# Up projection of a gated MLP: high and low parts of the operand in one matmul of 512 columns for four of a step's seven products

## The chip, the cores and the metric

The kernel runs on one core of a Trainium2 chip. The metric is the device time of one execution in microseconds (us); it was measured in three runs of the kernel before, and one more execution was recorded by the hardware profiler. TensorE (PE in the profile) does the matmuls and loads their weights (PEld), VectorE (DVE) and ScalarE (ACT) do elementwise work, GpSimd (POOL) and SyncE (SP) here mostly start DMAs.

## The reference, cut to what matters

The reference is one transformer block over 512 tokens of width 2048 in fp32: attention and a short convolution, then a gated MLP with a convolution of three taps along the tokens. The change lies in the MLP, in its first product `h @ w_up`:

```python
D_MODEL = 2048; SEQ = 512
FFN_DIM = ((8 * D_MODEL // 3 + 127) // 128) * 128      # 5504 = 43 * 128

def dwconv3(x, w, b):
    xp = jnp.pad(x, ((0, 0), (1, 1), (0, 0)))
    return xp[:, :-2] * w[0] + xp[:, 1:-1] * w[1] + xp[:, 2:] * w[2] + b

def conv_ffn(h, w_up, cw, cb, w_down):
    u = dwconv3(h @ w_up, cw, cb)
    a, g = jnp.split(u, 2, axis=-1)
    return (a * jax.nn.silu(g)) @ w_down

hf_l = modulate(rms_norm(x, g_ffn_norm[l]), sh_f, sc_f)
x = x + gt_f * conv_ffn(hf_l, w_up[l], ffn_conv_w[l], ffn_conv_b[l], w_down[l])
```

## The kernel before

Every fp32 operand of TensorE is split in two: a rounded part (`h`, high) and what is left (`l`, low). A product is made of three matmuls on top of each other in one bank, `mm3` (lines 185 to 189): high weights with high activations (L187), high weights with low activations (L188), low weights with high activations (L189).

The width 2048 of the normed activations lies in 16 tiles `hf0` to `hf15` of 128 partitions and 512 tokens, each as a high and a low tile. The 43 column tiles of `a` and the 43 of `g` form 43 steps f. The first three are made by plain rows of matmuls over 512 tokens (names `uf`). The other 40 (f = 3 to 42, the loop that begins near line 1199) use a Strassen scheme, in which the tokens are halved (256 each), the width is halved (even and odd tiles) and the two column tiles of the step, one of `g` and one of `a`, are the third pair. A step then needs seven products instead of eight, each over 8 blocks of width and 256 columns: 7 x 8 x 3 = 168 matmuls of 256 columns. The products are named by their activations:

- p1 on "11" (first half of the tokens of the even `hf`), p2 on "21" (first half of the odd `hf`), p6 on "2" and q5 on "1" (sums of halves, the tiles `T`), p7 on "3" (a sum stored over the second half of the even `hf`). These five run in step f itself.
- q4 on "4" (a `T` tile) and q3 on "22" (second half of the odd `hf`) of step f run within step f+1, in `finish`, between p2 and p6 of that step.

Weights of a product come as one tile of 128 x 1024 (eight blocks). `split4` casts them to high on ACT (L998) and subtracts on VectorE for low (L999); there are three buffers each for high and low. In the trace `u27q4h` is the high part of the weights of product q4 of step 27, and u27a, u27b, u27c are the three banks of step 27: a collects p1, p6, p7 and q4, b is p2's, c collects q5 and q3. After p1, p6 and p7 ACT copies bank a aside (L1174). VectorE adds the pieces into the tiles `cg` and `ca` (L1212, L1224, L1182; L1180 on ACT). Then come the convolution (`conv3`: L1005 on ACT, L1006 and L1007 on VectorE), silu (L1013) and the product of `a` and `g` (L1015).

The weights of a step are five tiles: 11, 12, 22, and the sums s1 and s3. SP loads all five (L1119) into nine buffers; for s1 and s3 POOL then starts a second DMA that adds onto the loaded tile (L1121, 512 KB). VectorE makes two more sums from them (L1213, L1214).

The results of two steps make a pair. From f = 7 on, `pair_sums` (L1031 to L1061) writes seven operands of each pair to memory for the down projection, one `put` after another; each call of `pump(1)` behind a product asks for the next one. A put is a cast on ACT (L1042), a subtraction on VectorE (L1043) and a DMA of 256 KB started by POOL (L1044) to `t_d`. The seven, in order, are called #1 to #7 here: "11", "1", "3", "22", "2", "21", "4". In the trace `tp922` is the put of pair 9 (steps 25 and 26) for the operand "22". The tile `tp` of a put comes from the same 58 buffers as `hf` (32) and `T` (24), so two are left: #6 takes the buffer of #4, #7 that of #5, and the second put of the next pair that of #7. POOL starts its DMAs in the order of its instructions, so puts and the adding DMAs of the weights stand in one line.

The order on each engine is not written by hand. A scheduler with an estimate of each instruction's time arranges the program when it is built.

Of the kernel before, what the change touches and what calls it, by code (L numbers as in the profile page):

```python
# [10 lines left out]
F32 = mybir.dt.float32  # L11
F32R = mybir.dt.float32r
# [60 lines left out]
def block_kernel(ctx, tc, xt, ctxt, ctxn, c, c_ctx, w_ada, small, w_in, w_inc, w_q, w_kv, w_out,  # L73
# [23 lines left out]
    def t2(shape, dt, name):  # L97
        return act.tile(shape, dt, tag="t2", bufs=NT2, name=name)
# [80 lines left out]
    def part(w, i, n=1):  # L179
        return tuple(z[:, i * P:(i + n) * P] for z in w)  # L180
# [4 lines left out]
    def mm3(ps, w, x, first, last, on_top=False):  # L185
        with tc.issue_after(behind.pop()) if behind else ExitStack():
            PE.matmul(ps, w[0], x[0], start=first, stop=False, skip_group_check=on_top)  # L187
        PE.matmul(ps, w[0], x[1], start=False, stop=False, skip_group_check=on_top)  # L188
        PE.matmul(ps, w[1], x[0], start=False, stop=last, skip_group_check=on_top)  # L189


    bg, post, late_bg = deque(), [], []
# [437 lines left out]
    with ExitStack() as pb:  # L630
# [238 lines left out]
        def bank_of(i, nm):  # L869
            return p8.tile([P, 512], F32, tag=f"s{i}", bufs=1, name=nm)  # L870
# [41 lines left out]
    def whole(raw, xs, nm, ps=None, cols=slice(0, T), ld=None, often=False):  # L912
# [10 lines left out]
            pump(1)  # L923
        return ps

    hf = {}


    hf_last = [None, None]

    def hf_tile(j, cols=slice(0, T)):
        if j not in hf:
            hf[j] = tuple(t2([P, T], F32R, f"hf{j}{z}") for z in "hl")
        sc = tiny(1, f"fs{j}")
        scale_of(sc, s("g_ffn", j), mod[:, 64 + j:65 + j])
        xr = xres[j][:, cols]
        with tc.issue_after(hf_last[0]) if hf_last[0] is not None else ExitStack():
            V.tensor_tensor(out=xr, in0=xr, in1=rl[:, cols], op=ALU.mult)
        A.activation(xr, xr, AF.Identity, bias=mod[:, 48 + j:49 + j], scale=sc)
        hi, lo = (z[:, cols] for z in hf[j])  # L940
        A.copy(out=hi, in_=xr)
        ins = V.tensor_tensor(out=lo, in0=xr, in1=hi.bitcast(F32), op=ALU.subtract)
        hf_last[:] = hf_last[1], ins.ins

    def hf_early():
# [129 lines left out]
    def t_sums(j):  # L1075

        e, o = xres[2 * j], xres[2 * j + 1]
        i, c = j // 2, HS[j % 2]
        if j % 2 == 0:
            for n in (1, 2, 4):  # L1080
                TT[n, i] = tuple(t2([P, T], F32R, f"T{n}{i}{z}") for z in "hl")

        def put(dst, src):
            hi, lo = dst
            A.copy(out=hi, in_=src)
            V.tensor_tensor(out=lo, in0=src, in1=hi.bitcast(F32), op=ALU.subtract)

        V.tensor_tensor(out=e[:, H0], in0=e[:, H0], in1=e[:, H1], op=ALU.subtract)
        V.tensor_tensor(out=e[:, H1], in0=o[:, H1], in1=e[:, H1], op=ALU.subtract)
        put(half_of(hf[2 * j], 1), e[:, H1])  # L1090
        V.scalar_tensor_tensor(out=o[:, H1], in0=e[:, H0], scalar=-1.0, in1=o[:, H1], op0=ALU.mult, op1=ALU.subtract)
        V.scalar_tensor_tensor(out=o[:, H0], in0=o[:, H1], scalar=-1.0, in1=o[:, H0], op0=ALU.mult, op1=ALU.subtract)
        for n, src in ((1, e[:, H0]), (2, o[:, H1]), (4, o[:, H0])):
            put(tuple(z[:, c] for z in TT[n, i]), src)

    def operand(n, j):
        if n in ("11", "3"):
            return half_of(hf[2 * j], n == "3")
        if n in ("21", "22"):
            return half_of(hf[2 * j + 1], n == "22")  # L1100
        return half_of(TT[int(n), j // 2], j % 2)

    def first_weights(k, held=False):

# [8 lines left out]
    def up_load(f):  # L1113
# [7 lines left out]
                G_.dma_start(r[-1], src[more], accum_op=ALU.add)  # L1121
        return r

    pss = [bank_of(i, f"uf{g}") for g, i in enumerate((2, 3, 4, 5, 1, 0))]
    held = [first_weights(k, k > 2) for k in range(EARLY)]
    for k in range(3, EARLY):
        hf_tile(k, H0)
    for k in range(EARLY):
        row(pss, held[k], hf[k], k, H0)
        pump(1)  # L1130
    drain()
    for k in range(EARLY):
        hf_tile(k, H1)
        row(pss, held[k], hf[k], k, H1)
        pump(1)
        if k in (3, 5):
            t_sums(k // 2 - 1)
# [9 lines left out]
    for k in range(EARLY, NK):  # L1147
        w = nxt
        if k + 1 < NK:
            if k == NK - 4:  # L1150
                raws = up_load(G // 2)
            if k == NK - 2:
                t_sums(sums.popleft())
            nxt = prepare(k + 1)
        row(pss, w, hf[k], k)
        if k % 2:
            sums.append(k // 2)
            t_sums(sums.popleft())
# [3 lines left out]
    bank8 = in_turn(BANKS)  # L1162
    one_bank[0] = bank8

    def product(ps, a, n, nm, first):

        w = split4(a, 1024, nm)
        for j in range(8):
            mm3(ps[:, :256], part(w, j), operand(n, j), first and j == 0, j == 7, on_top=not first)
        pump(1)  # L1170

    def aside(ps, nm):
# [4 lines left out]
    def finish(st):  # L1177
        f, a22, s4, u2, u3, pa, pc, cg, ca = st
        product(pa, a22, "4", f"u{f}q4", False)
        A.activation(ca[:, H0], pa[:, :256], AF.Identity, scale=-1.0)  # L1180
        product(pc, s4, "22", f"u{f}q3", False)
        V.tensor_tensor(out=cg[:, H1], in0=pc[:, :256], in1=u2, op=ALU.add)  # L1182
        acts(f, cg, ca)


# [13 lines left out]
    for f in range(G // 2, NF):  # L1199
        a11, a12, s1, s3, a22 = raws  # L1200
        if f + 1 < NF:
            raws = up_load(f + 1)
        else:
            for _ in range(AHEAD):
                plain_fetch()
        pa, pb, pc = (bank8(f"u{f}{z}") for z in "abc")
        cg = cp.tile([P, T], F32, tag="cg", bufs=2, name=f"cg{f}")
        ca = cp.tile([P, T], F32, tag="ca", bufs=2, name=f"ca{f}")
        product(pa, a11, "11", f"u{f}p1", True)
        u1 = aside(pa, f"u{f}1")  # L1210
        product(pb, a12, "21", f"u{f}p2", True)
        V.tensor_tensor(out=cg[:, H0], in0=pb[:, :256], in1=u1, op=ALU.add)  # L1212
        V.tensor_tensor(out=a11, in0=a11, in1=s1, op=ALU.add)  # L1213
        V.tensor_tensor(out=a12, in0=a12, in1=a11, op=ALU.add)  # L1214
        if pend is not None:
            finish(pend)
        if first_acts and f == G // 2:
            acts(*first_acts.pop(0))
        product(pa, a11, "2", f"u{f}p6", False)
        u2 = aside(pa, f"u{f}2")  # L1220
        product(pc, s1, "1", f"u{f}q5", True)
        product(pa, s3, "3", f"u{f}p7", False)
        u3 = aside(pa, f"u{f}3")
        V.scalar_tensor_tensor(out=ca[:, H1], in0=pc[:, :256], scalar=-1.0, in1=u3, op0=ALU.mult, op1=ALU.subtract)  # L1224
        if first_acts:
            acts(*first_acts.pop(0))
        pend = f, a22, a12, u2, u3, pa, pc, cg, ca
# [366 lines left out]
```

## Time and profile before

| | us |
|---|---|
| median of 3 runs | 2148.93 |
| lowest and highest | 2143.85, 2150.8 |
| the profiled execution | 2158.83 |
| its span, first to last instruction | 2157.0 |

| engine | busy, us | share of the span |
|---|---|---|
| TensorE, matmul | 2104.9 | 98% |
| TensorE, weight load | 1946.7 | 90% |
| VectorE | 1769.0 | 82% |
| ScalarE | 1047.1 | 49% |
| GpSimd | 188.1 | 9% |

The 40 steps lie between about 820 and 1685 us of the span. In the rows of a timeline the first number is the start, the second the duration in us, then follow the engine, the line in the kernel, the operation, and what is written from what; in brackets stands how long the engine was idle before and what ended that. A matmul's shown duration runs until its result is out, so that neighbours overlap; the pace is read from one start to the next. In a row of DMA issues the last number is the time from issue to landing.

### The profile page before, as it was taken

How to read it: one execution, taken by the hardware profiler on the slowest of the kernel's cores; microseconds unless marked ns; L12 is line 12 of the kernel's file. 1: busy time of each engine (PE TensorE's matmuls, PEld its weight loads, DVE VectorE, ACT ScalarE, POOL GpSimd, SP SyncE). 2: the span in 40 equal slices, each digit the busy share in tenths (PEclk: the TensorE clock that was granted, in tenths of full speed). 3: DMA queues.
4: the chain of work that ended last, by engine and by line, in shares of the span. 5: the costliest groups of instructions: out<-in, count | busy, mean ns of one | idle time of the engine just before them, and what ended most of it. 6: DMA issues, size and time to landing. Idle time of an engine off the chain costs nothing.

```text
span 2157.0 us, 37744 instructions
## 1 busy us (share of the span) xinstructions
PE 2104.9 (98%) x14458; PEld 1946.7 (90%) x14458; DVE 1769.0 (82%) x2859; ACT 1047.1 (49%) x1710; POOL 188.1 (9%) x270
## 2 busy tenths in 40 slices
PE   7899999999999999999999999999999999999997
PEld 4688788888888888999999999999999889999997
DVE  7998987778886889788888788788888658888877
ACT  5533333555552237555555555555555333333445
POOL 0000000000000000111211111111111000000000
PEclk9999999999999999999999999999999999999998
DMA  9979785334559986577887877877887999877683
GB/s 335 345 275 337 270 279 176 128 126 162 177 199 348 344 278 192 159 217 201 241 232 215 240 229 220 237 231 219 241 229 218 341 335 290 254 220 236 196 247 111
DMA packets 162121, 513.89 MB, mean 238 GB/s; under 512 B 18962, under 2 KB 23314, under 8 KB 156306
## 3 DMA queue, kind: packets, MB, share of 16 engines
q1 hardware_dynamic: 133364, 418.14, 56.5%
q0 software_dynamic: 27488, 92.29, 18.3%
q8 instruction: 113, 1.85, 0.3%
q10 hardware_dynamic: 1088, 1.05, 0.1%
q14 instruction: 68, 0.56, 0.1%
HBM read 464.22 MB, written 46.14 MB: 237 GB/s over the span
## 4 chain that ended last, share of the span: by engine, by line
PE 86%; DVE 6%; DMA 5%; issue 1%; ACT 1%; SPq 0%; DVEq 0%; POOLq 0%; ACTq 0%
PE pp L187 4%; PE pp L189 4%; PE pp L188 4%; PE o L189 1%; PE o L187 1%; PE o L188 1%; DMA ada<-in_w_ada 1%; PE d L187 1%; PE d L189 1%; PE d L188 1%; PE uf L187 1%; PE uf L188 1%; PE of L187 1%; PE of L188 1%; PE of L189 1%
## 5 line engine op out<-in xcount | busy, mean ns | idle before, releaser
L1044 POOL DMA_DIRECT2D t_d<-tp x126 | 71.9, 574 | 468.3 <-DVE tp L1043 465.4
L255 DVE SCALAR_TENSOR_TENSOR ada<-ada,sv 128x1024 f32<-128x1024 f32 x68 | 82.1, 1219 | 12.1 <-DMA ada<-in_w_ada 12.0
L166 ACT CAST w_0h<-rw 128x512 fp32r<-128x512 f32 (+1 forms) x63 | 38.3, 618 | 108.3 <-PE pp L188 63.1
L1121 POOL DMA_DIRECT2D u_s<-in_w_up x80 | 70.2, 878 | 224.4 <-DMA u_s<-in_w_up 131.5
L233 DVE SCALAR_TENSOR_TENSOR ada<-ada,sv 128x1024 f32<-128x1024 f32 x64 | 77.5, 1217 | 4.4 <-DMA ada<-in_w_ada 3.9
L522 DVE SCALAR_TENSOR_TENSOR ada<-ada,svc 128x1024 f32<-128x1024 f32 x64 | 76.0, 1220 | 2.3 <-DMA ada<-in_w_ada 2.3
L785 POOL TENSOR_TENSOR gr<-gr,half 128x8 f32<-128x8 f32 x4 | 10.1, 2524 | 628.7 <-DVE gr L784 536.8
L1042 ACT CAST tp<-a 128x256 fp32r<-128x256 f32 x90 | 34.7, 405 | 60.5 <-DMA t_d<-tp 54.1
L167 DVE TENSOR_TENSOR w_0l<-rw,w_0h 128x512 fp32r<-128x512 f32 (+1 forms) x63 | 42.6, 681 | 22.3 <-ACT w_0h L166 22.3
L255 DVE SCALAR_TENSOR_TENSOR ra<-ra,sv 128x1024 f32<-128x1024 f32 x44 | 52.5, 1217 | 1.1 <-DMA ra<-in_w_ada 1.1
L1213 DVE TENSOR_TENSOR u<-u,u_s 128x1024 f32<-128x1024 f32 x40 | 48.8, 1219 | 0.7 <-DMA u_s<-in_w_up 0.7
L1214 DVE TENSOR_TENSOR u<-u,u 128x1024 f32<-128x1024 f32 x40 | 48.7, 1218 | 0.0
L1043 DVE TENSOR_TENSOR tp<-a,tp 128x256 fp32r<-128x256 f32 x90 | 36.2, 418 | 12.3 <-ACT tp L1042 12.3
L756 ACT CAST pth<-t 128x384 fp32r<-128x384 f32 x64 | 28.6, 485 | 26.4 <-PE t L753 26.4
L1042 ACT CAST tp<-ts 128x256 fp32r<-128x256 f32 x36 | 14.6, 407 | 43.5 <-DMA t_d<-tp 41.1
L533 DVE TENSOR_TENSOR acc<-acc,pp 128x512 f32<-128x512 f32 x50 | 34.0, 680 | 2.1 <-PE pp L189 2.1
L757 DVE TENSOR_TENSOR ptl<-t,pth 128x384 fp32r<-128x384 f32 x64 | 33.2, 549 | 2.7 <-ACT pth L756 2.7
L737 DVE TENSOR_REDUCE mn<-s 128x1 f32<-128x768 f32 x32 | 30.4, 952 | 4.8 <-PE s L726 4.6
L1043 DVE TENSOR_TENSOR tp<-ts,tp 128x256 fp32r<-128x256 f32 x36 | 15.2, 421 | 23.3 <-ACT tp L1042 23.3
L1005 ACT ACTIVATE g<-cg,sm 128x512 f32<-128x512 f32 x40 | 32.5, 813 | 0.5 <-DVE cg L1182 0.5
L1005 ACT ACTIVATE a<-ca,sm 128x512 f32<-128x512 f32 x40 | 32.1, 803 | 0.0
L1013 ACT ACTIVATE g<-g 128x512 f32<-128x512 f32 x43 | 27.2, 632 | 6.4 <-DVE g L1007 6.4
(15967 smaller groups left out, 9398.2 us busy)
## 6 DMA issues: line engine op xcount, KB each, us to landing
ada<-in_w_ada SPq DMA_DIRECT2D x196, 512.0 KB, 6.0
u<-in_w_up SPq DMA_DIRECT2D x120, 512.0 KB, 8.2
w<-t_d SPq DMA_DIRECT2D x161, 256.0 KB, 5.2
u_s<-in_w_up SPq DMA_DIRECT2D x80, 512.0 KB, 4.3
u_s<-in_w_up POOLq DMA_DIRECT2D x80, 512.0 KB, 8.9
t_d<-tp POOLq DMA_DIRECT2D x126, 256.0 KB, 4.9
v<-in_w_dnw SPq DMA_DIRECT2D x72, 384.0 KB, 5.4
ra<-in_w_ada SPq DMA_DIRECT2D x22, 1024.0 KB, 4.9
```

The lines of the kernel that those rows point to most:

```text
L187: PE.matmul(ps, w[0], x[0], start=first, stop=False, skip_group_check=on_top)
L188: PE.matmul(ps, w[0], x[1], start=False, stop=False, skip_group_check=on_top)
L189: PE.matmul(ps, w[1], x[0], start=False, stop=last, skip_group_check=on_top)
L233: V.scalar_tensor_tensor(out=r, in0=r, scalar=1.0, in1=vec[:, i * 1024:(i + 1) * 1024], op0=ALU.mult, op1=ALU.mult, accum_out=col[:, i:i + 1])
L255: keep(V.scalar_tensor_tensor(out=r, in0=r, scalar=1.0, in1=svs[i], op0=ALU.mult, op1=ALU.mult, accum_out=lc[:, t % 4:t % 4 + 1] if i else ...
L522: keep(V.scalar_tensor_tensor(out=raw[q], in0=raw[q], scalar=1.0, in1=svc[:, q * 1024:(q + 1) * 1024], op0=ALU.mult, op1=ALU.mult, accum_o ...
L1005: A.activation(u, src, AF.Identity, bias=s("fb", m), scale=s("fw", 86 + m))
L1042: A.copy(out=z[:, :256], in_=src)
L1043: V.tensor_tensor(out=z[:, 256:], in0=src, in1=z[:, :256].bitcast(F32), op=ALU.subtract)
L1044: G_.dma_start(t_d[p, OPS.index(n)], z.bitcast(F32))
L1121: G_.dma_start(r[-1], src[more], accum_op=ALU.add)
L1213: V.tensor_tensor(out=a11, in0=a11, in1=s1, op=ALU.add)
```

## The change

For four of the seven products (p2, q5, q4, q3; `APART`) the high and low parts of the operand lie side by side in one tile of 512 columns. A new `mm2` multiplies the high weights with both at once, one matmul of 512 columns: high times high falls into the first half of the bank, high times low into its second half. The low weights then meet the high part in a matmul of 256 columns. Two matmuls take the place of three. What lies in the bank's second half is added by VectorE: `beside`, four new additions or subtractions of 128 x 256 in each step, one behind each of the four products' results.

To have the parts side by side, the odd `hf` tiles and the `T` tiles are laid out by half of the tokens, high beside low. The plain rows of the first three column tiles then do their odd tiles in two halves: 36 matmuls of 256 columns in the place of 18 of 512.

```diff
+    def mm2(ps, w, x, first, last, on_top=False):
+        n = x.shape[1] // 2
+        with tc.issue_after(behind.pop()) if behind else ExitStack():
+            PE.matmul(ps[:, :2 * n], w[0], x, start=first, stop=False, skip_group_check=on_top)
+        PE.matmul(ps[:, :n], w[1], x[:, :n], start=False, stop=last, skip_group_check=on_top)
...
+    def side_by_side(z, src):
+        n = T // 2
+        A.copy(out=z[:, :n], in_=src)
+        return V.tensor_tensor(out=z[:, n:], in0=src, in1=z[:, :n].bitcast(F32), op=ALU.subtract)
...
-        hi, lo = (z[:, cols] for z in hf[j])
-        A.copy(out=hi, in_=xr)
-        ins = V.tensor_tensor(out=lo, in0=xr, in1=hi.bitcast(F32), op=ALU.subtract)
+        if j % 2 == 0:
...
+        else:
+            for h in range(2):
+                if cols in (HS[h], slice(0, T)):
+                    hf[j, h] = t2([P, T], F32R, f"hf{j}{h}")
+                    ins = side_by_side(hf[j, h], xres[j][:, HS[h]])
...
-        if j % 2 == 0:
-            for n in (1, 2, 4):
-                TT[n, i] = tuple(t2([P, T], F32R, f"T{n}{i}{z}") for z in "hl")
+        for n in (1, 2, 4):
+            TT[n, j] = t2([P, T], F32R, f"T{n}{j}")
...
+    def up_row(w, k, hs=(0, 1)):
+        if k % 2 == 0:
+            row(pss, w, hf[k], k, slice(hs[0] * 256, hs[-1] * 256 + 256))
+            return
+        for g in range(G):
+            for h in hs:
+                mm3(pss[g][:, HS[h]], w[g], two(hf[k, h]), False, k == NK - 1 and h == 1)
...
+    APART = ("21", "1", "4", "22")
+
+    def beside(dst, ps, minus=False):
+        V.tensor_tensor(out=dst, in0=dst, in1=ps[:, 256:], op=ALU.subtract if minus else ALU.add)
+
     def product(ps, a, n, nm, first):
         w = split4(a, 1024, nm)
         for j in range(8):
-            mm3(ps[:, :256], part(w, j), operand(n, j), first and j == 0, j == 7, on_top=not first)
+            x = operand(n, j)
+            if n in APART:
+                mm2(ps, part(w, j), x, first and j == 0, j == 7, on_top=not first)
+            else:
+                mm3(ps[:, :256], part(w, j), x if isinstance(x, tuple) else two(x), first and j == 0, j == 7, on_top=not first)
         pump(1)
...
         A.activation(ca[:, H0], pa[:, :256], AF.Identity, scale=-1.0)
+        beside(ca[:, H0], pa, True)
         product(pc, s4, "22", f"u{f}q3", False)
         V.tensor_tensor(out=cg[:, H1], in0=pc[:, :256], in1=u2, op=ALU.add)
+        beside(cg[:, H1], pc)
...
         V.tensor_tensor(out=cg[:, H0], in0=pb[:, :256], in1=u1, op=ALU.add)
+        beside(cg[:, H0], pb)
...
         V.scalar_tensor_tensor(out=ca[:, H1], in0=pc[:, :256], scalar=-1.0, in1=u3, op0=ALU.mult, op1=ALU.subtract)
+        beside(ca[:, H1], pc, True)
```

The change also shifts what the scheduler makes of the program. Lines are numbered higher in the changed kernel: the split is L1023 and L1024, the puts are L1067, L1068 and L1069, the adding DMA is L1144, `beside` is L1200, `mm2` is L196 and L197.

ScalarE in step 28, before, from the cast of p6's weights to the cast of the next step's p1; `ts9` and `a26` are sources of puts of pair 9, `g27` and `a27` begin the convolution of step 27:

```order
L998 CAST u28p6h_14765<-u28_11_14351 128x1024
L1042 CAST tp92_14681<-ts9_14525 128x256
L998 CAST u28q5h_14795<-u28_s1_14355 128x1024
L1180 ACTIVATE ca27_14367<-u27a_14363 128x256
L1042 CAST tp921_14716<-a26_14492 128x256
L998 CAST u28p7h_14823<-u28_s3_14358 128x1024
L1005 ACTIVATE g27_14755<-cg27_14366,sm_82 128x512
L1005 ACTIVATE a27_14760<-ca27_14367,sm_82 128x512
L998 CAST u29p1h_14871<-u29_11_14601 128x1024
```

The same stretch of ScalarE in the changed kernel:

```order
L1023 CAST u28p6h_14158<-u28_11_13793 128x1024
L1023 CAST u28q5h_14188<-u28_s1_13797 128x1024
L1221 ACTIVATE ca27_13809<-u27a_13805 128x256
L1067 CAST tp92_14087<-ts9_13946 128x256
L1023 CAST u28p7h_14208<-u28_s3_13800 128x1024
L1030 ACTIVATE g27_14148<-cg27_13808,sm_82 128x512
L1030 ACTIVATE a27_14153<-ca27_13809,sm_82 128x512
L1067 CAST tp921_14115<-a26_13913 128x256
L1023 CAST u29p1h_14257<-u29_11_14015 128x1024
```

Puts #5 (`tp92`) and #6 (`tp921`) stand about one product later; #6 now stands right ahead of the cast of p1's weights of step 29.

GpSimd around the adding DMAs of step 29 (`u29_s1`, `u29_s3`), before:

```order
L1044 DMA t_d_80<-tp93_14594 128x512
L1044 DMA t_d_80<-tp922_14646 128x512
L1121 DMA u29_s1_14605<-in_w_up 128x1024
L1044 DMA t_d_80<-tp92_14681 128x512
L1121 DMA u29_s3_14608<-in_w_up 128x1024
L1044 DMA t_d_80<-tp921_14716 128x512
L1044 DMA t_d_80<-tp94_14750 128x512
```

The same stretch of GpSimd in the changed kernel:

```order
L1069 DMA t_d_80<-tp93_14007 128x512
L1144 DMA u29_s1_14019<-in_w_up 128x1024
L1069 DMA t_d_80<-tp922_14060 128x512
L1144 DMA u29_s3_14022<-in_w_up 128x1024
L1069 DMA t_d_80<-tp92_14087 128x512
L1069 DMA t_d_80<-tp921_14115 128x512
L1069 DMA t_d_80<-tp94_14142 128x512
```

Put #4 (`tp922`) has moved from ahead of the adding DMA of s1 to behind it, and #5 from ahead of that of s3 to behind it.

TensorE at the passage from q4 to q3 of step 27, before:

```order
L187 MATMUL u27a_14363<-T43h_8334,u27q4h_14688 128x256
L188 MATMUL u27a_14363<-T43l_8335,u27q4h_14688 128x256
L189 MATMUL u27a_14363<-T43h_8334,u27q4l_14689 128x256
L187 MATMUL u27c_14365<-hf1h_7571,u27q3h_14721 128x256
L188 MATMUL u27c_14365<-hf1l_7572,u27q3h_14721 128x256
L189 MATMUL u27c_14365<-hf1h_7571,u27q3l_14722 128x256
```

The same passage in the changed kernel:

```order
L196 MATMUL u27a_13805<-T47_8497,u27q4h_14095 128x512
L197 MATMUL u27a_13805<-T47_8497,u27q4l_14096 128x256
L187 MATMUL u28a_14027<-T20_7910,u28p6h_14158 128x256
L188 MATMUL u28a_14027<-T20_7910,u28p6h_14158 128x256
L196 MATMUL u27c_13807<-hf11_7839,u27q3h_14121 128x512
L197 MATMUL u27c_13807<-hf11_7839,u27q3l_14122 128x256
```

Each group of three has become a group of two, and the first two matmuls of p6 of step 28 now stand ahead of q3. Put orders like these are found in 15 pairs of steps (f = 12 to 40).

More of the change, by code (lines that the diff above doesn't have):

```diff
@@ L926, in block_kernel, with two @@
     hf = {}
+    def side_by_side(z, src):
+        n = T // 2
+        A.copy(out=z[:, :n], in_=src)
+        return V.tensor_tensor(out=z[:, n:], in0=src, in1=z[:, :n].bitcast(F32), op=ALU.subtract)
+    def two(z):
+        return z[:, :T // 2], z[:, T // 2:]
     hf_last = [None, None]
     def hf_tile(j, cols=slice(0, T)):
-        if j not in hf:
+        if j % 2 == 0 and j not in hf:
             hf[j] = tuple(t2([P, T], F32R, f"hf{j}{z}") for z in "hl")
@@ L939, in hf_tile @@
         A.activation(xr, xr, AF.Identity, bias=mod[:, 48 + j:49 + j], scale=sc)
-        hi, lo = (z[:, cols] for z in hf[j])
-        A.copy(out=hi, in_=xr)
-        ins = V.tensor_tensor(out=lo, in0=xr, in1=hi.bitcast(F32), op=ALU.subtract)
+        if j % 2 == 0:
+            hi, lo = (z[:, cols] for z in hf[j])
+            A.copy(out=hi, in_=xr)
+            ins = V.tensor_tensor(out=lo, in0=xr, in1=hi.bitcast(F32), op=ALU.subtract)
+        else:
[3 more added lines that the diff above has]
+                    ins = side_by_side(hf[j, h], xres[j][:, HS[h]])
         hf_last[:] = hf_last[1], ins.ins
@@ L1077, in t_sums @@
         e, o = xres[2 * j], xres[2 * j + 1]
-        i, c = j // 2, HS[j % 2]
-        if j % 2 == 0:
-            for n in (1, 2, 4):
-                TT[n, i] = tuple(t2([P, T], F32R, f"T{n}{i}{z}") for z in "hl")
+        for n in (1, 2, 4):
+            TT[n, j] = t2([P, T], F32R, f"T{n}{j}")
         def put(dst, src):
@@ L1093, in t_sums @@
         for n, src in ((1, e[:, H0]), (2, o[:, H1]), (4, o[:, H0])):
-            put(tuple(z[:, c] for z in TT[n, i]), src)
+            put(two(TT[n, j]), src)
     def operand(n, j):
@@ L1099, in operand @@
         if n in ("21", "22"):
-            return half_of(hf[2 * j + 1], n == "22")
-        return half_of(TT[int(n), j // 2], j % 2)
+            return hf[2 * j + 1, int(n == "22")]
+        return TT[int(n), j]
     def first_weights(k, held=False):
@@ L1128, in block_kernel @@
     for k in range(EARLY):
-        row(pss, held[k], hf[k], k, H0)
+        up_row(held[k], k, (0,))
         pump(1)
@@ L1133, in block_kernel @@
         hf_tile(k, H1)
-        row(pss, held[k], hf[k], k, H1)
+        up_row(held[k], k, (1,))
         pump(1)
@@ L1154, in block_kernel @@
             nxt = prepare(k + 1)
-        row(pss, w, hf[k], k)
+        up_row(w, k)
         if k % 2:
```

## The prediction

> **What bounds the kernel now.** I read the page first (busy shares, then the chain that ended last), then the up projection's steps in a view of stretches, then timelines of one pair of steps, engine by engine.
>
> ```profile
> span 2157.0 us, 37744 instructions
> PE 2104.9 (98%) x14458; PEld 1946.7 (90%) x14458; DVE 1769.0 (82%) x2859; ACT 1047.1 (49%) x1710; POOL 188.1 (9%) x270
> PE 86%; DVE 6%; DMA 5%; issue 1%; ACT 1%; SPq 0%; DVEq 0%; POOLq 0%; ACTq 0%
> ```
>
> TensorE is busy in 98% of the span and makes 86% of the last chain. Two steps, from the first p6 matmul of step 27 to that of step 29 (columns: length, then busy us and count of PE, PEld, DVE, ACT, POOL, granted clock, DMA share, GB/s):
>
> ```profile
> 1374.06:1394.22 20.16, 20.16 (x170) 20.16 (x169) 16.29 (x22) 11.71 (x18) 3.45 (x6) 1.00 0.74 206
> 1394.22:1414.38 20.16, 20.16 (x170) 20.16 (x169) 17.05 (x24) 11.47 (x17) 3.90 (x6) 1.00 0.85 244
> ```
>
> The reader is to see that TensorE has no gap here at full granted clock, and that VectorE has 16.7 of 20.16 us filled. A step's 168 matmuls thus run at 20.16 / 168 = 120.0 ns each. So a cheaper matmul shortens the step one for one, and a late operand lengthens it one for one: nothing else covers it.
>
> **The change, part by part. The matmul.** Matmuls of 512 columns, in plain rows of the down projection (15 intervals), and a mixed group of the attention:
>
> ```profile
> 1716.26 0.39 PE L188 MATMUL d<-yl4l,dw04h 128*128 128x512 f32 x1
> 1719.74 0.39 PE L189 MATMUL d<-yl4h,dw04l 128*128 128x512 f32 x1
> ...
> 456.13 0.39 PE L722 MATMUL s<-kl01h,q01h 128*128 128x512 f32 x1
> 457.27 0.28 PE L722 MATMUL s<-kcx,q01h 128*128 128x256 f32 x1
> 457.87 0.40 PE L722 MATMUL s<-kl01h,q01h 128*128 128x512 f32 x1
> ```
>
> (1719.74 - 1716.26) / 15 = 232 ns for one of 512. In the mix five of 512 take 1.14 us and five of 256 take 0.60, 348 ns for one of each. Three of 256 cost 360.0 ns; a 512 and a 256 cost 352.0 by the first row and 348 by the second: the gain is 8 to 12 ns. I take 7.9 (232.1 + 120.0, the longer sample). There are 40 steps x 4 products x 8 blocks = 1280 groups: **-10.1 us** (to -15.4). The mix changes width both ways without an extra gap, so neither a loss nor a larger gain is expected of the alternation.
>
> The Trainium skill, "TensorE: Matmul & The Clock Gate", section "Back-to-back issue gap", gives N / 2.4 + 2.5 ns for an isolated warm matmul, and warns that the spacing of a stream depends on its weight loads too. By that formula (215.8 and 109.2 ns) a group would save only 2.5 ns, 1280 of them 3.2 us, and the forecast would be some 7 us higher. The trace has 120.0 and 232: its fixed part is 8 ns, not 2.5, and the trace decides.
>
> The plain rows of the first three column tiles lose the same way: 5 full odd rows x 18 x (240.0 - 232.1) = **+0.7 us**.
>
> **VectorE.** The four additions per step have the shape of these two:
>
> ```profile
> 1394.87 0.42 DVE L1182 TENSOR_TENSOR cg<-u27c,u 128x256 f32<-128x256 f32 x1
> 1395.21 0.41 DVE L1061 SCALAR_TENSOR_TENSOR a<-ts,a 128x256 f32<-128x256 f32 x1
> ```
>
> From start to start it is 0.34 us, so 4 x 0.34 = 1.4 us, at most 1.7 by full duration. 16.7 + 1.4 = 18.1 of a step of 20.16 - 0.25 = 19.91 us: covered by VectorE's own idle time, cost 0. Bounds: 0, and the second rival below.
>
> **The moved puts.** This is what I expect to decide. Times in brackets count from 1374.06. In the kernel before:
>
> ```profile
> 1383.02 1.05 ACT L998 CAST u27q4h<-u 128x1024 fp32r<-128x1024 f32 x1 [2.07 <-PE u27a L188]
> 1383.02 0.41 DVE L1051 TENSOR_TENSOR a<-a,a 128x256 f32<-128x256 f32 x1
> 1383.36 0.42 DVE L1056 SCALAR_TENSOR_TENSOR ts<-ts,a 128x256 f32<-128x256 f32 x1
> 1384.83 1.22 DVE L999 TENSOR_TENSOR u27q4l<-u,u27q4h 128x1024 fp32r<-128x1024 f32 x1
> 1386.07 2.46 SPq L1119 DMA_DIRECT2D u_s<-in_w_up  x2
> 1387.01 1.13 POOL L1044 DMA_DIRECT2D t_d<-tp  x2 [11.87 <-DVE tp L1043]
> 1390.49 0.89 POOL L1121 DMA_DIRECT2D u_s<-in_w_up  x1 [2.34 <-DMA u_s<-in_w_up]
> 1393.17 0.56 POOL L1044 DMA_DIRECT2D t_d<-tp  x1 [1.79 <-DVE tp L1043]
> 1392.01 0.41 ACT L1042 CAST tp<-ts 128x256 fp32r<-128x256 f32 x1 [2.36 <-DMA t_d<-tp]
> 1397.18 1.05 ACT L998 CAST u29p1h<-u 128x1024 fp32r<-128x1024 f32 x1 [0.33 <-PE u28a L188]
> 1399.98 0.28 PE L187 MATMUL u29a<-hf0h,u29p1h 128*128 128x256 f32 x1
> ```
>
> Read from top to bottom: u27q4l is done at 1386.05 [11.99], which frees a weight buffer; SP loads the s1 weights of step 29 into it at once (0.02 later); POOL waits for that load and starts the adding DMA at 1390.49, 4.42 after SP. Puts #3 and #4 have left long before, at 1387.01. ACT's cast for #5 waits 2.36 us for a buffer, but p1h of step 29 is cast 1.75 us before TensorE wants it (1398.23 to 1399.98). How long the transfers take from issue to landing: the put of 1387.01, the adding DMA of 1390.49, the put of 1393.17, and the median of all adding DMAs:
>
> ```profile
> t_d<-tp POOLq DMA_DIRECT2D x1, 256.0 KB, 4.9
> ...
> u_s<-in_w_up POOLq DMA_DIRECT2D x1, 512.0 KB, 9.7
> ...
> t_d<-tp POOLq DMA_DIRECT2D x1, 256.0 KB, 8.1
> ...
> u_s<-in_w_up POOLq DMA_DIRECT2D x80, 512.0 KB, 8.9
> ```
>
> A put started behind an adding DMA lands about when that does: 1393.17 + 8.1 = 1401.27, against 1400.19. With nothing ahead it needs 4.9.
>
> In the changed order #4 stands behind the adding DMA of s1, and the cast for #6, which takes #4's buffer, stands right ahead of p1h of step 29 on ACT. Step by step: L1051 and L1056 now stand behind u27q4l, which so ends 0.67 earlier, [11.3] (its high part, done at 1384.07, allows that). SP + 0.02, POOL + 4.42: the adding DMA at [15.75]. #4 is queued behind it, and lands with it: + 9.7, [25.45]; + 8.9 by the median, + 10.8 (1401.27 - 1390.49) by the put of this stretch. Then the cast of #6 and p1h, 0.31 and 1.05:
>
> ```profile
> 1401.32 0.41 ACT L1042 CAST tp<-a 128x256 fp32r<-128x256 f32 x1 [2.82 <-DMA t_d<-tp]
> 1401.63 0.63 ACT L1013 ACTIVATE g<-g 128x512 f32<-128x512 f32 x1
> ```
>
> p1h is ready at [26.8]. TensorE wants it at 19.91 + 22 x 0.12 (p6's first two matmuls have moved ahead) + 2.82 (q5, eight groups) = [25.4]. Stall: **1.45 us, from 0.65 to 2.55**. p7 of step 28 is queued behind the two early p1 matmuls, so it waits too.
>
> A second wait follows. #6's subtraction comes at [25.9] instead of [20.5]. Up to #7's on VectorE stand one of 256 columns, L1006 and L1007 (0.66 each), p1l (1.14), one of 256, L1015 (0.60), p2l and L1213 (1.14 each):
>
> ```profile
> 1396.68 0.74 DVE L1006 SCALAR_TENSOR_TENSOR g<-cg,sm,g 128x511 f32<-128x511 f32 x1
> 1397.34 0.74 DVE L1006 SCALAR_TENSOR_TENSOR a<-ca,sm,a 128x511 f32<-128x511 f32 x1
> ...
> 1401.76 0.42 DVE L1043 TENSOR_TENSOR tp<-a,tp 128x256 fp32r<-128x256 f32 x1 [1.22 <-ACT tp L1042]
> 1402.10 1.22 DVE L1213 TENSOR_TENSOR u<-u,u_s 128x1024 f32<-128x1024 f32 x1
> 1403.24 0.68 DVE L1015 TENSOR_TENSOR a<-a,g 128x512 f32<-128x512 f32 x1
> 1403.84 1.22 DVE L999 TENSOR_TENSOR u29p2l<-u,u29p2h 128x1024 fp32r<-128x1024 f32 x1
> 1402.48 0.54 POOL L1044 DMA_DIRECT2D t_d<-tp  x1 [6.67 <-DVE tp L1043]
> 1406.92 0.41 ACT L1042 CAST tp<-ts 128x256 fp32r<-128x256 f32 x1 [0.23 <-DMA t_d<-tp]
> ```
>
> Together 6.0: #7 at [31.9], on POOL 0.72 later, its buffer free 4.44 after that (1406.92 - 1402.48), [37.1]; then #2's cast (0.31) and p6h of step 29 (1.05), [38.4]. TensorE wants p6h at 39.82 - 2.82 (q3 now behind it) - 0.24 + 1.45 = [38.2]: **0.2 us**, from 0 to 0.4.
>
> So 1.7 us a pair (0.65 to 2.9), in the 15 pairs whose order changed: 15 x 1.7 = **+25.5 us** (+10 to +44).
>
> **Sum:** 25.5 - 10.1 + 0.7 = +16.1 us on the profiled execution's 2158.83, 2174.9. That execution lay 9.9 above the median, so the median forecast is 2148.93 + 16.1 = **2165.0**. Gain and stall balance at 9.4 / 15 = 0.63 us a pair.
>
> **The rivals.** *The put is not held.* If #4 lands 4.9 us after its issue at about [16.6], its buffer is free at [21.5], and #6's cast comes in time; only the matmul's gain is left: 2148.93 - 9.4 = 2139.5, faster. For it: puts with nothing ahead land in 4.9. Against: the put of 1393.17, issued 2.7 us behind an adding DMA, landed a microsecond after it. It decides where #4 lands less than 25.4 - 1.36 - 15.75 = 8.3 us after the adding DMA's issue; the median of those DMAs, 8.9, is not far off.
>
> *VectorE becomes the bound (slower).* Q3's first matmul must now wait until VectorE has read q5's part out of bank c (L1200), which stands behind q3's low part. By the rows that is at 11.3 + 0.67 + 0.34 + 1.14 + 2 x 0.34 = [14.1], TensorE wants the bank at about [17.0]. Should an addition that reads the bank's second half take 1.2 us instead of 0.34, VectorE's step would be 16.7 + 4.8 = 21.5 us, 1.6 longer than TensorE's, and the kernel 40 x 1.6 = 64 us longer, some 2204. The point is where an addition takes over (19.91 - 16.7) / 4 = 0.8 us. Row L1182 reads a bank with the same shape in 0.42, against it.
>
> *The group of two costs as much as three of 256.* Then nothing is won: 2149.6 without a stall, 2175 with it. The mixed rows speak against it.
>
> **How the numbers follow.** About 0.3% (6.4 us) is what a measurement here can tell from no change. The forecast has 0.70: its own range, 2150 to 2184, comes from 0.65 to 2.9 us a pair, and 1.05 us a pair is what 6.4 us slower needs, so 0.57 of it is slower and 0.13 the same. The put that is not held: 0.17 (0.14 faster, 0.03 the same). VectorE: 0.05 slower. No gain of the matmul: 0.05 (0.03 the same, 0.02 slower). The 0.03 left: 0.02 faster, 0.01 slower. Faster 0.16, same 0.19, slower 0.65. The range 2143 to 2187 leaves out most of the first rival below (its 0.14) and some 0.06 above.
>
> **What would show it.** In p2, q5, q4, q3 groups 352 ns apart, the steps up to 11 (no puts moved) 19.9 us long: the first term. One idle stretch of TensorE of 0.65 to 2.55 us per pair, ended by p1h on ACT, with a cast of `tp` ahead of it that waits for `t_d`: the second. A shorter one ahead of p6: the third. Pairs of steps then take some 41.5 us instead of 40.32. If TensorE shows no idle stretch there, the forecast's mechanism is wrong; if VectorE is full, the second rival is right.

## The result and the profile after

The changed kernel takes 2210.1 us (median of 4 runs, 2203.93 to 2214.06), the kernel before 2149.86 in the same comparison: a ratio of 1.0279 (95% interval 1.0242 to 1.0315). The forecast was 2165.0, with a range of 2143 to 2187. The direction and the place were right; the loss is nearly four times as large as predicted (60 us instead of 16). The profiled execution took 2214.06 us.

The page's first line, its busy shares and the chain that ended last, after:

```profile
span 2212.3 us, 35471 instructions
PE 2114.5 (96%) x13268; PEld 1900.1 (86%) x13268; DVE 1828.2 (83%) x3024; ACT 1051.6 (48%) x1715; POOL 187.7 (8%) x270
PE 66%; DMA 16%; DVE 10%; issue 4%; ACT 3%; POOL 0%; SPq 0%; DVEq 0%; POOLq 0%; ACTq 0%
```

TensorE made 86% of the last chain, now 66%; transfers made 5%, now 16%. The view of waits for TensorE, steps 3 to 42 (what waited, for what, us in all, times, longest), names the place; 15 of its 17 rows are for p1, one for each odd step from 13 to 41:

```profile
PE u25a L187 <- ACT u25p1h L1023: 4.0, 1, 4.0
...
PE u29a L187 <- ACT u29p1h L1023: 2.7, 1, 2.7
...
PE u37a L187 <- ACT u37p1h L1023: 2.2, 1, 2.2
```

In the kernel before, the same view has no wait in these steps at all. The first p6 matmuls of steps 27, 28 and 29 on TensorE:

```profile
1402.01 0.27 PE L187 MATMUL u27a<-T,u27p6h 128*128 128x256 f32 x1
...
1421.78 0.28 PE L187 MATMUL u28a<-T,u28p6h 128*128 128x256 f32 x1
...
1446.00 0.28 PE L187 MATMUL u29a<-T,u29p6h 128*128 128x256 f32 x1
```

Step 27 takes 19.77 us (20.16 before), step 28, which carries puts #4 to #7, takes 24.22. GpSimd and ScalarE in that stretch, then three rows of DMA landings (put #3, the adding DMA of s1, put #4):

```profile
1419.17 0.56 POOL L1069 DMA_DIRECT2D t_d<-tp  x1 [13.88 <-DVE tp L1068]
1420.68 0.86 POOL L1144 DMA_DIRECT2D u_s<-in_w_up  x1 [0.95 <-DMA u_s<-in_w_up]
1421.25 0.86 POOL L1069 DMA_DIRECT2D t_d<-tp  x1
...
1431.65 0.40 ACT L1067 CAST tp<-a 128x256 fp32r<-128x256 f32 x1 [3.45 <-DMA t_d<-tp]
1431.96 1.04 ACT L1023 CAST u29p1h<-u 128x1024 fp32r<-128x1024 f32 x1
...
t_d<-tp POOLq DMA_DIRECT2D x1, 256.0 KB, 5.7
...
u_s<-in_w_up POOLq DMA_DIRECT2D x1, 512.0 KB, 9.7
...
t_d<-tp POOLq DMA_DIRECT2D x1, 256.0 KB, 10.3
```

Put #3, ahead of the adding DMA, lands in 5.7 us; put #4, half a microsecond behind the adding DMA, in 10.3. ScalarE waits 3.45 us for #4's buffer with the cast of #6, and p1's weights of step 29 come after that. TensorE stood at the end of q5 since about 1430.24. What it did then, in stretches (length, then busy us and count of PE, PEld, DVE, ACT, POOL, granted clock, DMA share, GB/s), before, in and behind the idle stretch:

```profile
1426.95:1430.24 3.29, 3.29 (x22) 2.82 (x20) 2.15 (x3) 1.25 (x2) 0.00 (x0) 1.00 1.01 299
1430.24:1433.05 2.81, 0.16 (x2) 0.00 (x0) 0.96 (x2) 1.40 (x3) 0.24 (x1) 1.00 1.04 278
1433.05:1436.45 3.40, 3.40 (x16) 3.40 (x17) 3.40 (x6) 1.79 (x3) 0.30 (x1) 0.51 0.73 272
1436.45:1440.00 3.55, 3.55 (x30) 3.50 (x30) 3.46 (x5) 2.03 (x4) 0.54 (x1) 0.99 0.04 17
```

The granted clock column tells what the prediction did not reckon with. For 3.4 us behind the idle 2.81 us the clock is 0.51, and 16 matmuls of 256 columns pass where 28 would: 3.40 / 0.12 = 28. The stall costs 2.81 us and then 1.5 us more (3.40 - 16 x 0.12), with TensorE shown as busy. The Trainium skill, "TensorE: Matmul & The Clock Gate", section "What's actually happening", states that the clock falls to half after an idle window of about 3.4 us and comes back after as much sustained work. The return agrees with the trace; the drop comes sooner here, after 2.81 us.

Added up over steps 3 to 41 from the starts of all matmuls (time beyond 0.12 or 0.23 us up to the first start behind a wait is idle, the rest slow): 47.5 us idle, 20.8 us slow. From the first `uf` matmul to the first of the plain down projection the kernel takes 54.2 us longer (871.1 to 925.3). The terms: + 47.5 + 20.8 + 0.6 (plain rows, 69.07 to 69.65) - 15.6 (40 steps x 0.39) = 53.3.

### The profile page after: what moved, and what is told of

The parts are those of the page before. It is cut to its first block, busy times and chain, and to the rows that moved or that the text cites. A ratio compares the mean times of both kernels' runs of the same rounds, so it can differ in the third digit from the quotient of the medians.

```text
span 2212.3 us, 35471 instructions
## 1 busy us (share of the span) xinstructions
PE 2114.5 (96%) x13268; PEld 1900.1 (86%) x13268; DVE 1828.2 (83%) x3024; ACT 1051.6 (48%) x1715; POOL 187.7 (8%) x270
## 4 chain that ended last, share of the span: by engine, by line
PE 66%; DMA 16%; DVE 10%; issue 4%; ACT 3%; POOL 0%; SPq 0%; DVEq 0%; POOLq 0%; ACTq 0%
DMA t_d<-tp 8%; DMA u_s<-in_w_up 5%; PE pp L187 4%; PE pp L189 4%; PE pp L188 3%; PE o L187 1%; PE o L189 1%; PE o L188 1%; DMA ada<-in_w_ada 1%; PE uf L187 1%; PE uf L188 1%; PE of L187 1%; PE of L188 1%; PE d L187 1%; PE uf L189 1%
## 5 line engine op out<-in xcount | busy, mean ns | idle before, releaser
L1069 POOL DMA_DIRECT2D t_d<-tp x126 | 78.9, 627 | 525.6 <-DVE tp L1068 514.7
L1144 POOL DMA_DIRECT2D u_s<-in_w_up x80 | 69.8, 872 | 230.8 <-DMA u_s<-in_w_up 145.0
L1068 DVE TENSOR_TENSOR tp<-a,tp 128x256 fp32r<-128x256 f32 x90 | 37.7, 420 | 55.9 <-ACT tp L1067 55.9
L1067 ACT CAST tp<-a 128x256 fp32r<-128x256 f32 x90 | 34.7, 406 | 100.4 <-DMA t_d<-tp 93.6
L793 POOL TENSOR_TENSOR gr<-gr,half 128x8 f32<-128x8 f32 x4 | 10.1, 2522 | 630.2 <-DVE gr L792 538.3
L748 ACT ACTIVATE p<-s,mn 128x768 f32<-128x768 f32 x32 | 29.3, 915 | 1.6 <-DVE mn L745 1.3
L1294 DVE SCALAR_TENSOR_TENSOR aq<-aq,svq 128x512 f32<-128x512 f32 x32 | 21.3, 688 | 10.5 <-DMA aq<-in_w_ada 9.6
```

The lines of the kernel that those rows point to most:

```text
L1069: G_.dma_start(t_d[p, OPS.index(n)], z.bitcast(F32))
```

## The experiments

Theories at the start: **P**, the loss comes from put #4 standing behind the adding DMA of s1; **A**, the later place of the casts on ScalarE is enough for it; **V** and **L**, it comes from the additions on VectorE; **M**, from the matmul of 512 columns. All ratios are to runs of the kernel before made beside them. "Idle" and "slow" are sums over steps 3 to 41, counted as above.

**The order on GpSimd put back.** The adding DMAs are traced later, behind the last put.

```diff
             if more is not None:
-                G_.dma_start(r[-1], src[more], accum_op=ALU.add)
+                late_adds.append((r[-1], src[more]))
...
+    def add_onto():
+        dst, src = late_adds.popleft()
+        with tc.issue_after(last_put[0]) if last_put else ExitStack():
+            G_.dma_start(dst, src, accum_op=ALU.add)
```

It is called behind p1 and p2 in even steps, twice behind q5 in odd ones.

> The changed kernel, whole, with one order put back: the adding DMAs of s1 and s3 are traced behind puts #4 and #5, so GpSimd has #3 #4 s1 #5 s3 #6 #7 #1 #2 s1 s3 as before. Theory P (the loss comes from put #4 standing behind the adding DMA of s1 on GpSimd): no idle stretch of TensorE ahead of p1, every step 19.77 us, no slow clock, 40 x 0.39 = 15.6 us won and 0.6 lost in the plain rows: 2149.9 - 15 = 2135 us, ratio 0.993. Rival V (the four additions on VectorE and the wait for them are the loss): they are all still there, so 2195 to 2210 us. Rival A (the later place of the casts on ScalarE is enough for the loss): idle stretches of 1 us or more stay, 2160 us or more.

Measured: 2164.48 us, ratio 1.0050 (1.0037 to 1.0062); idle 14.6, slow 6.8. Two thirds of the idle time are gone (47.5 to 14.6) and most of the loss, but not all: theory P falls short by some 25 us. The number fits theory A too (it set 2160 us or more, with stretches above 1 us, and six are left). But A is not tested here, since ScalarE's order did not stay: the scheduler also moved #6's cast back ahead of that of p7's weights. GpSimd with puts #3 and #4 in one row and the adding DMA of s1, then ScalarE, in step 28:

```profile
1389.79 1.23 POOL L1070 DMA_DIRECT2D t_d<-tp  x2 [11.10 <-DVE tp L1069]
1391.32 0.89 POOL L1154 DMA_DIRECT2D u_s<-in_w_up  x1 [0.30 <-issue]
...
1397.85 0.41 ACT L1068 CAST tp<-a 128x256 fp32r<-128x256 f32 x1 [0.62 <-DMA t_d<-tp]
1398.16 1.04 ACT L1023 CAST u28p7h<-u_s 128x1024 fp32r<-128x1024 f32 x1
```

**The same order in the kernel before.** Put #4 is held behind the adding DMA of s1, #5 behind that of s3; nothing else is changed in the program.

```diff
+            at = {"22": -2, "2": -1}.get(n) if p < PAIRS - 1 and p > 1 else None
+            with tc.issue_after(adds[at]) if at else ExitStack():
-            G_.dma_start(t_d[p, OPS.index(n)], z.bitcast(F32))
+                G_.dma_start(t_d[p, OPS.index(n)], z.bitcast(F32))
```

> The kernel before, with three matmuls of 256 columns everywhere and no additions, but put #4 held behind the adding DMA of s1 and #5 behind that of s3 on GpSimd in every pair but the first two and the last. Theory P: the idle stretch ahead of p1 appears here too, about 2.8 to 3.1 us, followed by matmuls at half pace for 1.4 us more: 15 x 4.4 = 66 us, 2205 to 2225 us. Rivals V and M (the additions, or the matmul of 512 columns, are the loss): 2150 us.

Measured: 2199.71 us, ratio 1.0220 (1.0202 to 1.0239); idle 34.1, slow 18.1. Without the matmul of 512 columns and without one addition, the view of waits shows such a list too, p1 of the odd steps from 15 to 41, with two of its longest rows here:

```profile
PE u25a L187 <- ACT u25p1h L998: 2.8, 1, 2.8
PE u29a L187 <- ACT u29p1h L998: 2.5, 1, 2.5
```

Theory M falls, and V as the only cause. The stretches are a little shorter than expected (14 of 2.0 to 3.0 us), and so is the time. Theory A is still open: here too the scheduler followed the held puts on ScalarE and put #6's cast right ahead of that of p1's weights in 14 of the 15 pairs. In step 28:

```profile
1419.88 0.40 ACT L1043 CAST tp<-a 128x256 fp32r<-128x256 f32 x1 [4.36 <-DMA t_d<-tp]
1420.19 1.04 ACT L998 CAST u29p1h<-u 128x1024 fp32r<-128x1024 f32 x1
```

**No additions.** `beside` returns at once.

> The changed kernel without the four additions of a step (the bank's second half is left out of the result). The program's order then is that of before, puts and adding DMAs too. Theory P: 2135 us, the same as with the additions and the order put back, within 3 us: the additions cost nothing themselves, they only made the scheduler move the puts. Rival V: 2135 too, but then the kernel with the additions and the order of before lies at 2195 or more. No slow clock under P.

Measured: 2142.03 us, ratio 0.9942 (0.9926 to 0.9958); no idle stretch but one of 0.5 us in step 10, steps of 19.77. GpSimd and ScalarE have the orders of before in all 15 pairs. This is what the four products win while nothing is late, and it is 22 us less than the first experiment, which has the additions and a later cast of #5 on ScalarE.

**The layout alone.** `APART = ()`, no additions.

> Only the layout of the operands and the plain rows are changed: all seven products take three matmuls of 256 columns, no additions. Steps 20.16 us. The odd plain rows cost 90 x 8 ns = 0.7 us, at most 90 x 12 = 1.1: 2150.7 us, ratio 1.0003 by every theory; it measures the term alone, by the length of the plain rows.

Measured: 2148.36 us, ratio 0.9966 (0.9950 to 0.9982). The expectation missed: steps are 19.93 to 19.94 us, not 20.16. So more than half of the 0.39 us that a step gains does not come from the matmul of 512 columns.

**The puts put back on all three engines.** On top of the first experiment, the split of q4 in odd steps' `finish` is held behind put #5's source (L1084 in this run) on VectorE, that of q3 behind put #4's cast and subtraction.

```diff
+        if f > STD + 1 and f % 2:
+            held_up.append(sources["2"])
         product(pa, a22, "4", f"u{f}q4", False)
...
+        if f > STD + 1 and f % 2:
+            held_up.extend((casts["22"], subs["22"]))
         product(pc, s4, "22", f"u{f}q3", False)
```

> The changed kernel, whole, with the puts put back on all three engines: on GpSimd as in the first experiment, and on ScalarE and VectorE the sources, casts and subtractions of puts #3 and #4 ahead of the split of q3's weights, as before. Theory PA (the loss is the later place of the puts, on GpSimd and on ScalarE): puts #3 and #4 leave 7 us ahead of the next p6 as before, no idle stretch of TensorE, steps of 19.6 to 19.8 us, the time of the kernel without additions, ratio 0.994 to the kernel before (0.992 to 0.996). Rival V (what was left after the first experiment, 14.6 us of idle and 6.8 us of slow matmuls, is the additions' load on VectorE): idle stretches stay, ratio 1.002 to 1.006.

Measured: 2178.63 us, ratio 1.0122 (1.0101 to 1.0142); idle 27.1, slow 8.1. It is worse than the first experiment, and theory PA falls: GpSimd, ScalarE and VectorE have the puts in the order of the kernel without additions, and the loss is still there. Its rows in step 27, first ScalarE's cast of q4, then VectorE up to q4's low part, then SP's load and GpSimd's adding DMA of s1:

```profile
1388.29 1.05 ACT L1024 CAST u27q4h<-u 128x1024 fp32r<-128x1024 f32 x1 [2.04 <-PE u27a L188]
...
1387.06 1.23 DVE L1282 TENSOR_TENSOR u<-u,u_s 128x1024 f32<-128x1024 f32 x1 [1.17 <-DMA u_s<-in_w_up]
...
1389.94 1.22 DVE L1283 TENSOR_TENSOR u<-u,u 128x1024 f32<-128x1024 f32 x1
1391.07 0.42 DVE L1079 TENSOR_TENSOR a<-a,a 128x256 f32<-128x256 f32 x1
1391.41 0.42 DVE L1084 SCALAR_TENSOR_TENSOR ts<-ts,a 128x256 f32<-128x256 f32 x1
1391.74 1.22 DVE L1025 TENSOR_TENSOR u27q4l<-u,u27q4h 128x1024 fp32r<-128x1024 f32 x1
...
1392.99 2.46 SPq L1145 DMA_DIRECT2D u_s<-in_w_up  x2
...
1397.50 0.89 POOL L1156 DMA_DIRECT2D u_s<-in_w_up  x1 [2.44 <-DMA u_s<-in_w_up]
```

The high part is ready at 1389.34, the low part begins at 1391.74, 2.4 us later. In the kernel before that distance was 0.76 (1384.07 to 1384.83). VectorE comes late, and q4's low part frees the buffer for the next load of s1, so the adding DMA of s1 is late too; VectorE itself waits 1.17 us for the adding DMA of the step before. The rows thus form a ring: VectorE, q4's low part, load, adding DMA, VectorE. That the additions in VectorE's row lengthen it is argued from these rows; the narrow additions below test it.

**The clock, tested with a fill.** First the kernel to compare with: the changed kernel in its own late order of puts, held by hand, and p7's cast in even steps from 12 on held behind the cast of #6.

```diff
+        if 12 <= f <= 40 and f % 2 == 0:
+            held_up.append(casts["21"])
         product(pa, s3, "3", f"u{f}p7", False)
```

> The changed kernel with the puts in its own late order, held so by hand, and in even steps from 12 on the cast of p7's weights behind the cast of put #6 on ScalarE. It is the pair to the next one. All theories: the idle stretch of TensorE comes ahead of p7 (or of the early p1 matmuls beside it), 2.5 to 3.2 us in each of 15 pairs, and the matmuls after it stand 0.21 us apart for about 3.4 us: ratio 1.022 to 1.034.

Then the same with useless matmuls where TensorE would stand idle.

```diff
         product(pc, s1, "1", f"u{f}q5", True)
+        if 12 <= f <= 40 and f % 2 == 0:
+            for i in range(22):
+                PE.matmul(pb[:, :256], TT[1, 0][:, :128], TT[2, 0][:, :256], start=i == 0, stop=i == 21)
```

> The same with 22 useless matmuls of 256 columns behind q5 in those 15 steps, 22 x 0.12 = 2.64 us in all, in the place where TensorE would stand idle; their result is overwritten unread. Theory C (an idle stretch costs twice: the time itself, and 1.4 to 1.6 us because the granted clock is 0.5 for a while after it): the matmuls after the fill keep 0.12 us, and the kernel is 13 to 15 times 1.4 to 1.6 us shorter than the one without the fill, 18 to 24 us, although it does more. Rival T (the matmuls behind the idle stretch are slow because transfers or other engines are busy then): they stay slow, and the kernel is as long as without the fill or longer.

Measured: 2228.21 us, ratio 1.0351 (1.0334 to 1.0368) without the fill, a little above what was expected, since the idle stretches were 3.3 to 4.5 us; 2204.42 us, ratio 1.0237 (1.0218 to 1.0255) with it. With 330 matmuls more the kernel is 23.8 us shorter. Slow time falls from 28.3 to 6.3 us. The idle time itself is not what was saved: 58.1 us without the fill, 22.0 and 39.6 of fill (330 x 0.12) with it. (The fill also moved some puts and casts; three stretches of 2.2 to 2.5 us are left, with slow matmuls behind each.) The stretch of the idle time and the one behind it in step 28, without the fill and with it:

```profile
1436.82:1440.24 3.42, 0.04 (x1) 0.00 (x1) 1.91 (x3) 2.35 (x4) 0.54 (x1) 0.93 0.93 243
1440.24:1443.60 3.36, 3.36 (x17) 3.36 (x18) 3.36 (x5) 2.39 (x5) 0.00 (x0) 0.57 0.69 226
```

```profile
1426.62:1429.62 3.00, 2.79 (x25) 2.59 (x23) 2.19 (x4) 2.63 (x5) 0.57 (x1) 1.00 1.03 295
1429.62:1432.98 3.36, 3.36 (x28) 3.36 (x29) 3.36 (x6) 2.29 (x5) 0.00 (x0) 1.00 0.82 268
```

With the same engines busy and the transfers no fewer (268 against 226 GB/s), 28 matmuls pass instead of 17, at a granted clock of 1.00 instead of 0.57. Rival T falls: it is the idle stretch that slows what follows.

The kernel without the fill also settles theory A. On ScalarE its casts of #5 and #6 stand where the first experiment has them, behind that of q5's weights and ahead of that of p7's, in all 15 pairs; VectorE's row is the same too up to #5's subtraction in step 28. On GpSimd #4 stands behind the adding DMA of s1. In step 28:

```profile
1427.21 0.87 POOL L1150 DMA_DIRECT2D u_s<-in_w_up  x1 [1.02 <-DMA u_s<-in_w_up]
1427.77 0.86 POOL L1075 DMA_DIRECT2D t_d<-tp  x1
...
1437.89 0.40 ACT L1071 CAST tp<-a 128x256 fp32r<-128x256 f32 x1 [3.83 <-DMA t_d<-tp]
1438.20 1.04 ACT L1025 CAST u28p7h<-u_s 128x1024 fp32r<-128x1024 f32 x1
```

So with these casts in the same places, and p7's cast held there by hand in the one, the order on GpSimd makes the difference between a ratio of 1.0050 and one of 1.0351, and between 14.6 and 58.1 us of idle time. The late place of #6's cast ahead of p1's weights is not needed for the loss; it only decides which product waits.

**Narrow additions.** The kernel with the puts put back on all three engines (the one that its expectation calls "the first entry"), with additions of 16 columns.

```diff
-        V.tensor_tensor(out=dst, in0=dst, in1=ps[:, 256:], op=ALU.subtract if minus else ALU.add)
+        V.tensor_tensor(out=dst[:, :16], in0=dst[:, :16], in1=ps[:, 256:272], op=ALU.subtract if minus else ALU.add)
```

> The kernel of the fifth experiment list's first entry (all puts back where they were, on three engines), but each of the four additions takes 16 columns of the bank's second half instead of 256; the other 240 are left out of the result. Every wait of the additions stays, only their time on VectorE shrinks, by some 0.25 us each (estimate: 240 of 256 columns of a 0.34 us pace go, some of it is fixed). Theory V2 (what holds that kernel up is that VectorE's row has no room between the splits, so that q4's low part, and with it the load and the adding DMA behind it, come late): less than 5 us of idle in all, ratio 0.993 to 0.998. Rival W (the waits of the additions, the bank that they hold): 27 us idle as there, ratio 1.010 or more.

Measured: 2150.19 us, ratio 0.9993 (0.9976 to 1.0010); idle 7.7, slow 3.2. The same waits with less time on VectorE take away 28 us (2178.63 to 2150.19). Idle time and ratio lie a little above what V2 set, far from W: it is mostly the additions' time, and a rest of 11 us (0.9993 against 0.9942) remains beside the kernel without them: it belongs to the additions' waits and to the holds, which no run separates.

**Two products, p2 and q3; and q5 alone.** `APART` and the additions are cut to these.

> The change for two products alone, p2 and q3, with their two additions; the whole result. The scheduler leaves every put and adding DMA where it was before. Theory P+V (the loss is the moved puts, which the additions set off): no idle stretch of TensorE, steps of 19.8 to 19.9 us, ratio 0.994 to 0.998. Rival L (each addition costs by its load on VectorE, a quarter of the loss each): 2 x 14 us more, ratio 1.010 to 1.015.

> The change for one product alone, q5, with its one addition; the whole result. The scheduler moves the puts and adding DMAs as in the full change: #4 behind the adding DMA of s1. Theory P: nearly the whole loss, with a quarter of the additions: 15 idle stretches of 2 to 3.3 us ahead of p1 and slow matmuls behind most of them, ratio 1.018 to 1.030. Rival L: a quarter of the loss, ratio 1.003 to 1.009.

Measured: p2 and q3 with two additions, 2162.31 us, ratio 1.0035 (1.0021 to 1.0048), idle 7.4, slow 4.8; q5 alone with one addition, 2201.88 us, ratio 1.0220 (1.0198 to 1.0241), idle 39.9, slow 16.3. Its stretches are 1.6 to 4.0 us long, and slow matmuls follow only 8 of the 15. One addition that moves the puts costs far more than two that leave them. Yet two that leave them cost 12 us of idle and slow time, which P+V did not expect; the waits are for VectorE's low parts and for the cast of p1's weights. In step 28 ScalarE is late with that cast behind a wait of 1.10 us for an addition into `cg` (last row):

```profile
PE u23b L197 <- DVE u23p2l L1024: 1.1, 1, 1.1
...
PE u29a L187 <- ACT u29p1h L1023: 0.9, 1, 0.9
PE u37b L197 <- DVE u37p2l L1024: 0.9, 1, 0.9
...
1397.72 0.82 ACT L1030 ACTIVATE g<-cg,sm 128x512 f32<-128x512 f32 x1 [1.10 <-DVE cg L1200]
```

**Where the layout's gain comes from.** The kernel before with only the T tiles side by side, then with only the odd `hf` tiles (and the plain rows that go with them).

> The kernel before with one thing changed: high and low part of the T tiles (products p6, q5 and q4) side by side in one buffer. Nothing else moves. It asks where the shorter step of the layout alone comes from, 19.93 us against 20.16. If from where these operands lie: p6, q5 and q4 lose 0.23 / 7 x 3 = 0.10 us and the step is 20.06; if from the pace of the stream as a whole, all seven products change alike or none does: 19.93 or 20.16.

> The kernel before with one thing changed: high and low part of the odd hf tiles (products p2 and q3, and the odd plain rows) lie side by side by half of the tokens; T as before, three matmuls of 256 columns everywhere, no additions. T alone left the step at 20.16 us. If the shorter step of the whole layout comes from the odd hf tiles: 19.93 us here in every step, 40 x 0.23 = 9 us less, ratio 0.995 to 0.998. If only both together or something else of that program does it: 20.16 us, ratio 1.000.

Measured: T alone, a single run, 2155.01 us, steps of 20.16 us; `hf` alone 2145.8 us, ratio 0.9969 (0.9955 to 0.9984), steps of 19.93 to 19.94. All of the layout's gain comes with the odd `hf` tiles, yet the pace changes in all seven products: in this kernel a matmul takes 0.1187 us on average, 19.94 / 168, also in p1 and p7, whose operands are stored as before. Why is open.

With a complete result, the two layouts (0.9966 for all of it, 0.9969 for the odd `hf` tiles alone) are the only kernels here clearly below the kernel before; which of the two is faster can't be told from these runs.

## Why the prediction was wrong, point by point

- **The matmul, -10.1 us (to -15.4).** The groups of two stand 351 ns apart ((1418.97 - 1416.16) / 8 in p2 of step 28), as forecast (352), against 360 for three of 256 before. That is 11 us, and the products left as they were became faster too, which no term held: together 0.39 us a step, 15.6 us. But the reason given, the wider matmul, holds only in part. By the layout experiments 0.22 to 0.23 of the 0.39 is the stream's pace, which came with the `hf` layout; the groups of two then win 19.94 - 19.77 = 0.17 us a step, 6.8 us, 5.3 ns each instead of 7.9. That the term came out near its size was luck.
- **The plain rows, +0.7 us.** Measured 0.6.
- **VectorE, cost 0.** Wrong. The argument was a mean: 18.1 us of work in a step of 19.91. But the splits, puts and sums stand in one row, and in the steps with puts q4's low part is, by the rows shown above, on a ring with the loads. With the puts in their old order on GpSimd and ScalarE, additions and holds cost 36 us (2178.6 against 2142.0; the ratios 1.0122 against 0.9942 say 39), and 28 us of it go when the additions are narrow. The additions are also why the scheduler moved the puts: without them it did not. The rival on VectorE was given 0.05 and looked for the trouble at bank c and at an addition of 1.2 us; the additions took 0.42 as expected, and it was their place in the row that counted.
- **The stall, 1.45 us and 0.2, 15 times.** The mechanism and the place were right: the loss comes with the order on GpSimd, in either kernel. The size was not. The step that failed is "#4 is queued behind it, and lands with it: + 9.7". In pair 9 put #4 landed 1.2 us after the adding DMA (1421.25 + 10.3 against 1420.68 + 9.7), and its buffer was free for #6's cast 10.97 us after that DMA's issue (1431.65 - 1420.68); over 15 pairs it was 10.96 on average. The DMA itself came a little late: 9.56 us before TensorE had nothing left (1430.24 - 1420.68), 9.28 on average, where 25.4 - 15.75 = 9.65 was reckoned. So 1.45 + 0.09 + 1.27 = 2.81 in pair 9, and 3.07 on average (2.31 to 4.18), above the upper end of 2.55. The stalls were 46.1 us instead of 25.5. The second wait, ahead of p6, did not appear.
- **The other step that failed, with as large an error,** is the sentence "a late operand lengthens it one for one". Behind 13 of the 15 stalls the granted clock was halved for about 3.4 us, 1.4 us more a pair on average: 20.5 us that no term held.
- **The sum.** On the profiled executions it gave 2174.9, and 2214.06 was measured, 39.2 more: 20.6 of longer stalls, 20.5 of the clock and 1.4 of a wait in step 10 that was not forecast, less 5.5 that the steps won more, make 37.0.
- **The ends of the range.** Its upper end came from stalls of 44 us without a clock term; stalls of 46.1 and 20.5 of the clock lie beyond it.

## What to carry to other kernels

An idle stretch of TensorE above about 2 us should be priced with the slow matmuls that follow it, not by its length; a fill of useless matmuls is a quick test for that. An engine with a busy share of 83% on average can have no room at all at one place: look for the ring of waits that its row is part of, and price an added instruction there. And where a scheduler orders the program, the cheapest added instruction can move a transfer behind another: compare the orders of the queues first.

## What the runs showed of the hardware

The clock drop depends on more than the length of the idle stretch. In the runs here no step with less than 2.1 us of idle time had more than 1 us of slow matmuls behind it, and every one with more than 2.9 had; between them both happen (2.15 us with it in step 30 of the kernel before with the puts moved, 2.85 without it in step 18 of the kernel with q5 alone). The Trainium skill, "TensorE: Matmul & The Clock Gate", section "What's actually happening", calls the window of the gate free-running, not started by the kernel's work; the spread fits that, but no run here shows the window itself. The slow time was 1.4 to 1.6 us in most cases, 2.7 in some. The pace of a whole stream of matmuls of 256 columns went from 120.0 to 118.7 ns with the layout of some of their operands, also in products that do not use these operands. In p1 of steps 12 to 40 the intervals behind the three matmuls of a group were 117.5, 120.0 and 122.5 ns on average before, and 118.8, 118.5 and 118.7 with the odd `hf` tiles side by side; no run here shows why.
